# A two-layer decoder trunk on one core: the order of all instructions from a recorded list schedule in place of an online planner, and masked matmul steps at half width

## The chip, the core and the metric

The kernel runs on one core of one Trainium2 chip. The metric is the device time of one execution in microseconds (us); the time before is the median of three runs. One further execution was profiled: its trace gives, for every instruction, the engine, the start and the duration. The engines are PE (TensorE: matmuls and weight loads), DVE (VectorE), ACT (ScalarE), POOL (GpSimd) and SP (the engine that issues most DMAs).

## The reference, cut to what matters

Two layers over 2048 tokens of width 1024, all float32. Layer 0 is a gated DeltaNet with 8 heads (key width 128, value width 256), layer 1 a gated linear attention (GLA) with 4 heads of the same widths. Each layer projects its input, mixes along time, gates, projects back and normalises:

```
def gated_delta_rule(q, k, v, g, beta):
    ...
    A = jnp.where(strict, jnp.einsum('bhncd,bhnsd->bhncs', kb, k) * decay, 0.0)
    uw = lax.linalg.triangular_solve(A + eye, rhs, left_side=True, lower=True, unit_diagonal=True)
    ...
    def step(S, inp):
        v_new = u_n - jnp.einsum('bhcd,bhde->bhce', w_n, S)
        o = jnp.einsum('bhcd,bhde->bhce', qd_n, S) + jnp.einsum('bhcs,bhse->bhce', qk_n, v_new)
        S = S * gl_n[..., None, None] + jnp.einsum('bhcd,bhce->bhde', kd_n, v_new)
...
    x = layer_norm(DEEP_ALPHA * x + y, ln_g[i], ln_b[i])
```

Layer 0 also puts a causal convolution of four taps and a SiLU on q, k and v. GLA has the same recurrence without the triangular solve, with a decay per channel that makes its attention matrix a sum over levels of block pairs.

## The kernel before

**Tiling.** The tokens come in four groups of 512, each of four chunks of 128. A unit is one head of one layer on one group: 32 DeltaNet and 16 GLA units, in the order of `PHASES` (line 942): DeltaNet groups 0 and 1, GLA group 0, DeltaNet 2, GLA 1, DeltaNet 3, GLA 2, GLA 3. So there are seven changes of group.

**The work of a unit** is written as four kinds of steps.

- `gemms` (line 433) projects the inputs. Both operands are split into a high and a low part in float32r, and each product is three matmuls (`mm3`, line 235): by channel with 512 moving columns, by token with 256. The weights come in chunks through `wc` (16 buffers, line 933). The first time, a chunk is loaded raw (`wraw`), split by ACT and POOL and stored to DRAM as `wk`; later it is loaded split. The inputs `xh`, `xl` (8 buffers each) are reloaded at each change of group (`load_x`, line 377) through `woraw`, whose four buffers serve the output weights and the norm parameters too. Results leave PSUM through three buffers "g".
- `gdn_prep` (line 575) and `gla_prep` (line 677) prepare the chunk matrices in plain float32. DeltaNet inverts a unit triangular matrix: blocks of 16 by a loop of 15 steps on DVE (line 633), fed by a DMA that spreads the blocks over the partitions (`Arep`, line 627), and then doublings with matmuls. The doubling from 16 to 32 (lines 643 to 652) multiplies full 128x128 matrices and masks the result; those to 64 and 128 work on the blocks alone. GLA fills its attention matrix level by level; four levels (line 745) multiply full matrices and copy under a mask.
- `gdn_chain` and `gla_chain` (lines 790 and 815) run the recurrence over four chunks. Each DeltaNet chunk goes through PE, DVE, PE, ACT, PE and DVE in turn (`S`, `Rt`, `wt`). `chains` (line 828) then transposes the output.
- `outs` (line 855) multiplies by the output weights and, after a layer's last head, normalises. It has one PSUM buffer "o".

**The order.** The four kinds are generators that run as threads (line 929). `Plan.note` (line 70) estimates for each instruction when it ends, from the formulas of `COST` (line 131): for DVE 110 ns and 1.04 ns per element, for ACT 110 and 0.84, for POOL 90 and 2.35, and 800 ns until another engine may use the result. Each `yield` names a time; `Plan.run` (line 99) goes on with the first thread that is due on the planned clock of PE. Fixed times (`O_GAP`, `R_SLACK`, `AHEAD`, `Y_WAIT`) space some steps. The instructions are issued to the framework at once, in this order, and it may still reorder them; one instruction is pinned (`keep_in_program_order`, line 638).

Of the kernel before, what the change touches and what calls it, by code (L numbers as in the profile page):

```python
# [16 lines left out]
P = 128  # L17
# [33 lines left out]
class Plan:  # L51
# [3 lines left out]
    def __init__(self):  # L55
        self.clock = 0.0
        self.events = {}
        self.busy = dict.fromkeys("vsgd", 0.0)
        self.done, self.used, self.opens, self.slots = {}, {}, {}, {}

    def tile(self, tag, ap, bufs):
        slots = self.slots.setdefault(tag, [])
        slots.append(ap.tensor.name)
        self.opens[slots[-1]] = self.used.get(slots[-1 - bufs], 0.0) if len(slots) > bufs else 0.0

    def ready(self, *tiles):
        names = [t[:].tensor.name for t in tiles]
        return max(max(self.done.get(n, 0.0), self.opens.get(n, 0.0)) for n in names)

    def note(self, key, aps):  # L70
        dst, src = aps[0], aps[1:]
        names = [a.tensor.name for a in aps]
        t = max([self.opens.get(names[0], 0.0)] + [self.done.get(n, 0.0) for n in names[1:]])
        n = 1
        for k in (src[-1] if key == "t" else dst).shape[1:]:
            n *= k
        psum = any(a.space == PSUM for a in aps)
        if key == "t":
            m = 1
            for k in src[0].shape[1:]:  # L80
                m *= k
            rate = 0.6 if src[0].dtype == F32 else 2.4
            cost = m / 1.2 if src[0] is src[-1] else max(n / rate, m / rate, 107 if rate > 1 else 53)
            self.clock = end = max(self.clock, t) + cost
            end += COST["t"]
        else:
            if key == "d":
                cost, wait = COST["d"], COST["dw"] + 4 * n * P / 200
            else:
                fixed, each = COST[key]  # L90
                cost, wait = fixed + n * each, COST["w"]
            begin = max(self.busy[key], t)
            self.busy[key] = max(self.busy[key], min(begin, self.clock)) + cost
            end = begin + cost + wait
        self.done[names[0]] = max(end, self.done.get(names[0], 0.0))
        for a in names:
            self.used[a] = max(end, self.used.get(a, 0.0))

    def run(self, *threads, start):
        def due(th):  # L100
            return self.events.get(th[1], 1e30) if isinstance(th[1], tuple) else th[1]

        threads = [[t, t0] for t, t0 in zip(threads, start)]
        while threads:
            th = next((th for th in threads if due(th) <= self.clock), None) or min(threads, key=due)
            assert due(th) < 1e30
            self.clock = max(self.clock, due(th))
            try:
                th[1] = next(th[0])
            except StopIteration:  # L110
                threads.remove(th)


class Planned:
    def __init__(self, plan, engine, key):
        self.plan, self.engine, self.key = plan, engine, key

    def __getattr__(self, name):
        op = getattr(self.engine, name)

        def call(*args, **kw):
            ins = op(*args, **kw)  # L122
            aps = [a for a in (*args, *kw.values()) if isinstance(a, bass.AP)]
            if name == "transpose":
                aps = [aps[0], aps[1], aps[1]]
            self.plan.note(self.key, aps)
            return ins
# [7 lines left out]
def trunk(ctx, tc, x, xT, w_in1, conv, a_log, dt_bias, nw1, w_out1, w_in2, gk_up, gk_b, nw2, w_out2,  # L135
          ln_g, ln_b, consts, out, phases=None):
    nc = tc.nc
    plan = Plan()
    v, s, g = (Planned(plan, e, k) for e, k in ((nc.vector, "v"), (nc.scalar, "s"), (nc.gpsimd, "g")))
    pe, sync, acts = Planned(plan, nc.tensor, "t"), Planned(plan, nc.sync, "d"), Planned(plan, nc.scalar, "d")  # L140
    ready, events = plan.ready, plan.events
# [10 lines left out]
    def T(tag, shape, bufs=1, dt=F32, p=None):  # L152
        count[0] += 1
        t = (p or sb).tile(list(shape), dt, tag=tag, name=f"{tag}_{count[0]}", bufs=bufs)
        plan.tile(tag, t[:], bufs)
        return t
# [87 lines left out]
    def after(*names):  # L244
        for name in names:
            yield name

    def mark(*name):
        events[name] = plan.clock

    def prefetched(specs, load, ahead=1):
        ready = []
        specs = iter(specs)

        def take(ahead=ahead):
            while len(ready) <= ahead:
                spec = next(specs, None)
                ready.append(None if spec is None else load(spec))
            return ready.pop(0)
        return take  # L260

    class Stream:

        def __init__(self, specs):
            self.specs = iter(specs)
            self.chunks = {}
            self.taken = self.loaded = 0
            self.kept = {}  # L270

        def load(self, freed):
            while self.loaded < freed + W_BUFS:
                spec = next(self.specs, None)
                if spec is None:
                    return
                w, cols, kc, key, last = spec
                wc = T("wc", [P, 2, 272], W_BUFS, F32R)
                n = sum(2 * cn if pair else cn for c0, cn, pair in cols)
                if key in self.kept:  # L280
                    sync.dma_start(wc[:, :, :n].bitcast(F32), self.kept[key][:, :, :n])
                    self.chunks[self.loaded] = wc, None
                else:
                    raw = T("wraw", [P, 272], RAW_BUFS)
                    rows = w[kc * P:(kc + 1) * P]
                    n = 0
                    for c0, cn, pair in cols:
                        if pair:
                            sync.dma_start(raw[:, :2 * cn].rearrange("p (a b) -> p a b", a=2),
                                           rows[:, :2 * pair].rearrange("p (a b) -> p a b", a=2)[:, :, c0:c0 + cn])  # L290
                            n = 2 * cn
                        else:
                            sync.dma_start(raw[:, n:n + cn], rows[:, c0:c0 + cn])
                            n += cn
                    split(wc[:, 0, :n], wc[:, 1, :n], raw[:, :n], g)
                    keep = None
                    if not last:
                        keep = self.kept[key] = T("wk_%d_%d_%d_%d" % key, [P, 2, n], p=dr)
# [684 lines left out]
```

## Time and profile before

| what | value |
|---|---|
| three runs | 3163.24, 3164.54, 3171.97 us; median 3164.54 |
| profiled execution, own time | 3160.78 us |
| its span, first to last instruction | 3159.0 us |
| instructions in the trace | 51501, of them 18430 matmuls |
| mean granted TensorE clock | 0.989 |
| DMA traffic | 551.86 MB, 175 GB/s in the mean |

A row of a profile gives the engine, the operation with its output and inputs, the shape (stationary rows*columns, then moving partitions x elements), the count, the busy time with the mean duration, and idle time ahead of it with what ended it. All instructions have line 122, a helper's, so groups are told apart by tiles. A matmul's end is modelled: it is drawn longer than the time after which the next one can start. The pitch, from one matmul's start to the next, is what counts. A float32 matmul shows as two matmul instructions.

### The profile page before, as it was taken

Reading aid. Unit: us, or ns where it says so; the run is one execution under the profiler, and the core shown is the slowest. Engines: PE = TensorE matmul, PEld = TensorE weight load, DVE = VectorE, ACT = ScalarE, POOL = GpSimd, SP = SyncE. Lnnn points to the kernel's source line nnn. Section 1 sums busy time; section 2 is a strip of 40 time slices with the busy share of each in tenths; the row PEclk is TensorE's granted clock in tenths of the full one; section 3 lists DMA queues with packets and bytes.
Section 4 is the critical chain, followed back from the end, with each engine's and each line's share of the span. In section 5 each row is a group of like instructions: output and inputs, shape, how many; then the busy total and the mean of one; then the engine's idle time right before and its main releaser. Section 6 shows DMA issues by size and latency. Waiting matters only on the chain. (4 is left out here: it accounts for less than half of the span.)

```text
span 3159.0 us, 51501 instructions
## 1 busy us (share of the span) xinstructions
PE 3035.0 (96%) x18430; PEld 2591.3 (82%) x18430; DVE 2047.3 (65%) x4780; ACT 1184.4 (37%) x3091; POOL 519.2 (16%) x834
## 2 busy tenths in 40 slices
PE   8899999999999998999999999999999999999997
PEld 6678888778888887887888888888788888898886
DVE  5777777666666575567666657457866674745565
ACT  5445453343333445334233333423323332433331
POOL 5423330020001334002000001000200000200021
PEclk9999999999999999999999999999999999999998
DMA  7876665564444648655455444654645454455443
GB/s 238 258 230 220 191 216 185 165 214 138 141 147 152 212 132 280 215 175 196 135 157 161 142 149 134 206 179 154 198 151 154 139 161 132 157 188 170 151 161 107
DMA packets 442480, 551.86 MB, mean 175 GB/s; under 512 B 37568, under 2 KB 381888, under 8 KB 430192
## 3 DMA queue, kind: packets, MB, share of 16 engines
q1 hardware_dynamic: 412656, 505.57, 51.1%
q10 hardware_dynamic: 29568, 43.00, 3.9%
q8 instruction: 145, 2.38, 0.3%
q14 instruction: 111, 0.91, 0.1%
HBM read 421.24 MB, written 127.21 MB: 174 GB/s over the span
## 5 line engine op out<-in xcount | busy, mean ns | idle before, releaser
L122 PE MATMUL psg<-xh,wc 128*128 128x512 f32 x2560 | 890.1, 406 | 4.5 <-ACT wc L122 2.4
L122 PE MATMUL psg<-wc,xh 128*128 128x256 f32 (+1 forms) x4096 | 795.6, 291 | 10.0 <-POOL wc L122 2.5
L122 PEld LDWEIGHTS psg<-wc,xh 128*128 128x128 f32 x4096 | 658.8, 190 | 44.0 <-POOL wc L122 4.4
L122 PE MATMUL psg<-wc,xl 128*128 128x256 f32 (+1 forms) x2048 | 581.2, 284 | 0.4 <-DVE xl L122 0.4
L122 PEld LDWEIGHTS psg<-xh,wc 128*128 128x128 f32 x2560 | 482.1, 189 | 115.4 <-POOL wc L122 4.4
L122 PE MATMUL psg<-xl,wc 128*128 128x512 f32 x1280 | 514.8, 402 | 0.8 <-DVE xl L122 0.8
L122 PE MATMUL pso<-wo,oth 128*128 128x512 f32 x1472 | 505.1, 420 | 5.3 <-DVE y L122 4.6
L122 DVE SCALAR_TENSOR_TENSOR y<-pso,z,y 128x512 f32<-128x512 f32 x368 | 274.2, 745 | 193.8 <-PE pso L122 188.2
L122 PEld LDWEIGHTS psg<-wc,xl 128*128 128x128 f32 x2048 | 389.7, 190 | 1.8 <-DVE xl L122 0.9
L122 DVE SCALAR_TENSOR_TENSOR acc<-pb,taps,acc 128x512 f32<-128x512 f32 x384 | 302.8, 791 | 95.0 <-ACT acc L122 88.1
L122 PE MATMUL pso<-wo,otl 128*128 128x512 f32 x736 | 297.4, 404 | 0.0
L122 PEld LDWEIGHTS pso<-wo,oth 128*128 128x128 f32 x1472 | 254.3, 190 | 48.0 <-DVE y L122 13.0
L122 POOL TENSOR_TENSOR wc<-wraw,wc 128x256 fp32r<-128x256 f32 (+1 forms) x288 | 233.8, 825 | 323.5 <-ACT wc L122 313.2
L122 PEld LDWEIGHTS psg<-xl,wc 128*128 128x128 f32 x1280 | 242.2, 189 | 51.7 <-DVE xl L122 2.0
L122 ACT ACTIVATE junk<-psc 128x128 bf16<-128x128 f32 (+1 forms) x448 | 143.7, 321 | 230.0 <-PE psc L122 186.0
L122 ACT ACTIVATE th<-psg 128x256 f32<-128x256 f32 (+1 forms) x256 | 108.6, 436 | 254.2 <-PE psg L122 224.4
L122 ACT ACTIVATE D<-D 128x512 f32<-128x512 f32 x160 | 98.5, 630 | 212.5 <-DVE D L122 200.5
L122 PEld LDWEIGHTS pso<-wo,otl 128*128 128x128 f32 x736 | 138.8, 189 | 32.5 <-DVE otl L122 1.7
L122 DVE SCALAR_TENSOR_TENSOR sg<-th,psg 128x256 f32<-128x256 f32 x192 | 79.3, 417 | 124.0 <-ACT th L122 96.6
L122 ACT COPY pb<-psg 128x512 f32<-128x512 f32 x128 | 74.8, 584 | 224.6 <-PE psg L122 208.6
L122 ACT CAST wc<-wraw 128x256 fp32r<-128x256 f32 (+1 forms) x288 | 113.4, 406 | 121.0 <-PE psg L122 59.4
L122 DVE TENSOR_TENSOR Xt<-Arep,X 128x60 f32<-128x60 f32 (+14 forms) x480 | 103.3, 215 | 32.0 <-DMA Arep<-blk 22.0
(170 smaller groups left out, 4320.4 us busy)
## 6 DMA issues: line engine op xcount, KB each, us to landing
wc<-wk SPq DMA_DIRECT2D x816, 256.0 KB
wk<-wc SPq DMA_DIRECT2D x272, 256.0 KB
wraw<-in_w_in SPq DMA_DIRECT2D x288, 128.0 KB
wo<-ok_in_w_out SPq DMA_DIRECT2D x24, 1024.0 KB
wo<-k_in_w_out SPq DMA_DIRECT2D x24, 1024.0 KB
wo<-_in_w_out SPq DMA_DIRECT2D x22, 1024.0 KB
Arep<-blk SPq DMA_DIRECT2D x32, 512.0 KB
wc<-wk SPq DMA_DIRECT2D x48, 272.0 KB
```

Of the source, the lines that this page charges most:

```text
L122: ins = op(*args, **kw)
```

## The change

`Plan` and the threads go. Every instruction is recorded first (`Recorder.note`) with the tile regions that it reads and writes, then `place` decides the order of all of them, and `emit` issues them in that order, each pinned. `place` is a list scheduler: five queues (PE, DVE, ACT, POOL, and SP for DMAs), each takes the ready instruction of best rank: the chain first, then preparation, output, and projections last. An instruction that is the first to use a tile waits for a free buffer, in the order of the program within its rank, and its unit may be at most two ahead of the first unit whose chain is unfinished. The durations have new formulas per engine and operation; the result counts as there after a lag and 100 ns more (`SLACK`), 200 ns more for PE; a DMA lands 3500 ns and size/170 after its issue, `Arep` after 9000.

```diff
+        if key == "t":
+            mov = size_of(every[2].shape) if op.name == "matmul" else size_of(every[1].shape)
+            if op.name == "transpose":
+                op.cost = 2 * dst.shape[0] / 2.4 + 4
+            elif every[1].dtype == F32:
+                op.cost = 4 * mov / 2.4 + 9
+            else:
+                op.cost = mov / 2.25 + 4.5
+            op.lag = 210
+        elif key == "d":
+            size = 4 * n * dst.shape[0]
+            op.cost, op.lag = 430, DMA_LAG + size / 170
+            if isinstance(dst, View) and dst.of.tag == "Arep":
+                op.lag = REP_LAG
...
+        elif key == "v":
+            n = max(n, max(size_of(a.shape) for a in every))
+            took = (150 if psum else 160) + 1.04 * n
+            if op.name == "scalar_tensor_tensor":
+                took += 55
+            if len(every) > 2 and not psum and n > 64:
+                took *= 1.12
+            op.cost, op.lag = took - 80, 80 + LAG
+        elif key == "s":
+            took = (165 if psum else 210) + 0.833 * n
...
+            op.cost, op.lag = took - 95, 95 + LAG
         else:
...
+            took = 140 + 2.8 * n if len(every) > 2 else 300 + n
+            if op.args[-1] == ALU.pow:
+                took = 450 + 160 * n
+            op.cost, op.lag = took - 40, 40 + LAG
...
+            placed.append(op)
+            for u in op.users:
+                u.ready = max(u.ready, now + cost if u.deps[op] else end + (100 if u.key == "t" else 0) + SLACK)
...
+        for op in self.place():
+            tc.keep_in_program_order(op.call(*[real(a) for a in op.args], **{k: real(a) for k, a in op.kw.items()}))
...
-COST = {"v": (110, 1.04), "s": (110, 0.84), "g": (90, 2.35), "w": 800, "t": 200, "d": 450, "dw": 2000}
+LAG = 60
+DMA_LAG, REP_LAG, SLACK = 3500, 9000, 100
```

The masked steps work on the later half of each block pair alone: the stationary operand keeps its 128 columns, the moving one has 64, and the DVE steps on the result have 256 elements in place of 512.

```diff
+    def later_half(a, sz):
...
+        return a.rearrange("p n (m h j) -> p n m h j", h=2, j=sz)[:, :, :, 1, :]
...
-        d = PS("c", [P, NC, P])
-        yield ready(d, U)
+        Uh, Wh = later_half(U[:], 16), halves(W2[:, :, :P // 2], 16)
+        d = halves(PS("c", [P, NC, P // 2]), 16)
         for n in range(NC):
-            mm(d[:, n], A[:, n], U[:, n])
-        v.tensor_tensor(W2[:], d, bc(C(C_LV + 4), 1, NC), ALU.mult)
...
+            mm(d[:, n], A[:, n], Uh[:, n])
+        v.tensor_tensor(Wh, d, bc(later_half(C(C_LV + 4), 16), 1, NC), ALU.mult)
+        d = halves(PS("c", [P, NC, P // 2]), 16)
         for n in range(NC):
-            mm(d[:, n], Tm[:, n], W2[:, n])
-        v.tensor_tensor(U[:], U[:], d, ALU.subtract)
+            mm(d[:, n], Tm[:, n], Wh[:, n])
+        v.tensor_tensor(Uh, Uh, d, ALU.subtract)
...
+                d = halves(d, half)
+                E3 = E[:].rearrange("p (n t) -> p n t", n=NC)
                 for n in range(NC):
-                    c = slice(n * P, (n + 1) * P)
-                    mm(d[:, n], E[:, c], E[:, c])
-                v.copy_predicated(At[:], bc(C(C_LV + lv), 1, NC).bitcast(I32), d)
+                    mm(d[:, n], E3[:, n], later_half(E3, half)[:, n])
+                v.copy_predicated(later_half(At[:], half), bc(later_half(C(C_LV + lv), half), 1, NC).bitcast(I32), d)
```

Buffers and queues move too. Inputs get raw buffers of their own, two of them, and a load claims its `xh` and `xl` with its raw buffer; the output weights keep two raw buffers, the norm parameters get four. The stores of scaled output weights go from ACT's queue to SP's. The store of a split weight chunk no longer waits for the chunk's last use. The last unit's transposed output goes to `oth` and `otl` as every other unit's does. The loads of `y` lose their fixed delay; by rank they stand ahead of the projections' loads.

```diff
     def load_x(u, kc):
...
-        raw = T("woraw", [P, TG], WO_RAW_BUFS)
-        sync.dma_start(raw[:], x2T[u.gi][:, kc, :] if u.kind else xT[kc * P:(kc + 1) * P, u.t0:u.t0 + TG])
+        raw = T("xraw", [P, TG], 2)
         hi, lo = T("xh", [P, TG], KC, F32R), T("xl", [P, TG], KC, F32R)
+        sync.dma_start(raw[:], x2T[u.gi][:, kc, :] if u.kind else xT[kc * P:(kc + 1) * P, u.t0:u.t0 + TG],
+                       also=(hi, lo))
...
-            acts.dma_start(k[:], t[:].bitcast(F32))
...
+            sync.dma_start(kept_wo[key][:], t[:].bitcast(F32))
...
-                hi = T("D1" if end else "oth", [P, NC, P], 2, F32R)
+            hi = T("oth", [P, NC, P], 2, F32R)
...
-    plan.run(chains(), preps(), outs(), gemms(), start=(0.0, 0.0, 1.0, 0.0))
+    for u in units:
+        rec.unit = u.at
+        gemms(u)
+        preps(u)
+        chains(u)
+        outs(u)
+    rec.emit(tc)
...
-W_BUFS, RAW_BUFS = 16, 4
-WO_BUFS, WO_AHEAD, WO_RAW_BUFS = 2, 1, 4
+W_BUFS, RAW_BUFS = 14, 3
+WO_BUFS, WO_RAW_BUFS = 2, 2
...
-O_GAP = 7050
-R_SLACK, AHEAD = 2500, 500
-Y_WAIT = 20000
+R_CHAIN, R_PREP, R_OUT, R_GEMM = range(4)
+HORIZON = 2
```

More of the change, by code (lines that the diff above doesn't have):

```diff
@@ L262, in trunk @@
[L262 to L298, printed above, removed]
-                    self.chunks[self.loaded] = wc, keep
-                self.loaded += 1
-        def take(self):
-            self.taken += 1
-            return self.taken - 1, self.chunks.pop(self.taken - 1)
@@ L517, in short_conv @@
+        if not u.first:
+            gate(DV)
     def short_conv(d, blk):
@@ new lines, in chains @@
+    def chains(u):
+        rec.rank = R_CHAIN
+        og, ssq = T("og", [P, NC, DV], 1), small("ssq", NC)
+        (gdn_chain if u.kind == 0 else gla_chain)(u, og, ssq)
+        z = small("z", NC)
+        if u.kind == 1:
+            rsqrt(z[:], ssq[:], DV * 1e-6)
+        else:
+            v.tensor_tensor(ssq[:], ssq[:], u.prep["qn"][:], ALU.add)
+            rsqrt(z[:], ssq[:], 0.0)
+        u.z = z
+        u.oT = []
+        for j in range(2):
+            d = PS("c", [P, NC, P])
+            transposes(d, lambda n: og[:, n, j * P:(j + 1) * P], NC)
+            hi = T("oth", [P, NC, P], 2, F32R)
+            lo = T("otl", [P, NC, P], 2, F32R)
+            split(hi[:], lo[:], d)
+            u.oT.append((hi, lo))
```

713 lines of the change are left out of this document (398 added, 315 removed).

## The prediction

> **What bounds the kernel now.** I read the page first, then the groups by shape, the chain that ended last, the timeline, stretches of time, and the waits of PE's loads.
>
> ```profile
> span 3159.0 us, 51501 instructions
> ## 1 busy us (share of the span) xinstructions
> PE 3035.0 (96%) x18430; PEld 2591.3 (82%) x18430; DVE 2047.3 (65%) x4780; ACT 1184.4 (37%) x3091; POOL 519.2 (16%) x834
> ```
>
> PE looks 96% busy: 124 us of the span are idle. But ends of matmuls are modelled, so part of each wait is drawn as work. The pitch, start to start, tells what PE needs:
>
> ```profile
> 2285.41 5.60 PE psg L122 x24
> ...
> 2307.34 3.19 PE psg L122 x27
> ```
>
> ```profile
> 493.42 1.05 PE L122 MATMUL psc<-U,D 128*128 128x128 f32 x8
> ...
> 499.54 0.59 PE L122 MATMUL psc<-U,D 128*32 128x32 f32 x16
> ...
> 510.95 1.03 PE L122 MATMUL psc<-kq 128*128 128x256 f32 x4
> ```
>
> The first two rows are unbroken projection work: 5.60/24 = 233 ns with 512 moving columns, 3.19/27 = 118 ns with 256. In float32 the last matmul's drawn length comes off first (284, 199 and 381 ns in the groups): (1.05-0.284)/7 = 110 ns with 128 columns, (0.59-0.199)/15 = 26 ns with 32, (1.03-0.381)/3 = 216 ns with 256.
>
> ```profile
> L122 PE MATMUL psg<-xh,wc 128*128 128x512 f32 x2560 | 890.1, 406 | 4.5 <-ACT wc L122 2.4 <-POOL wc L122 1.2 <-ACT xh L122 0.7
> L122 PE MATMUL psg<-wc,xh 128*128 128x256 f32 x3584 | 690.1, 290 | 6.9 <-DVE sg L122 2.3 <-ACT vt L122 1.7 <-ACT wc L122 1.6
> L122 PE MATMUL psg<-xl,wc 128*128 128x512 f32 x1280 | 514.8, 402 | 0.8 <-DVE xl L122 0.8
> L122 PE MATMUL psg<-wc,xl 128*128 128x256 f32 x1792 | 505.5, 282 | 0.0
> L122 PE MATMUL pso<-wo,oth 128*128 128x512 f32 x1472 | 505.1, 420 | 5.3 <-DVE y L122 4.6
> L122 PE MATMUL pso<-wo,otl 128*128 128x512 f32 x736 | 297.4, 404 | 0.0
> L122 PE MATMUL psc<-S,qd 128*128 128x256 f32 x384 | 115.4, 382 | 0.6 <-DVE qn L122 0.6
> ...
> L122 PE MATMUL psc<-D 128*128 128x128 f32 x512 | 68.6, 277 | 2.8 <-DVE otl L122 2.4 <-DVE D L122 0.3
> ...
> L122 PE MATMUL psc<-cst,og 128*128 128x128 f32 x384 | 58.8, 275 | 9.9 <-DVE og L122 8.4 <-DVE D L122 1.5
> L122 PE MATMUL psh<-vt,kd 128*128 128x256 f32 x128 | 41.2, 404 | 7.7 <-DVE S L122 7.6
> L122 PE MATMUL psc<-vt,D 128*128 128x256 f32 x128 | 39.4, 390 | 0.8 <-ACT D L122 0.8
> ...
> L122 PE MATMUL psc<-W,Tm 128*128 128x128 f32 x256 | 35.6, 284 | 3.5 <-DVE W L122 3.5
> L122 PE MATMUL psc<-U,D 128*128 128x128 f32 x256 | 35.5, 284 | 7.6 <-DVE U L122 7.6
> ```
>
> Counts by pitch: 6048 of 512 columns (and 96 in small groups) by 0.232 are 1425 us. 6144 of 256 (768 of them slightly wider) by 0.118 to 0.125 are 730. 1920 in float32 with 256 columns (eight groups, the first and last shown) by 0.216 are 415. The 1024 masked ones (`D`, `W,Tm`, `U,D`) by 0.110 are 113, 1104 transposes by 0.109 are 120, and 2100 small ones some 106. The sum is 2909 us: PE needs 2909 of 3159 and loses 250, twice what the page shows as idle. This is the whole of what an order can win. Where it is lost:
>
> ```profile
> 0.00:200.00 200.00, 174.47 (x932) 139.72 (x932) 131.68 (x283) 93.98 (x264) 88.95 (x131) 0.96 0.81 254
> 200.00:3100.00 2900.00, 2821.26 (x17322) 2420.22 (x17323) 1879.85 (x4438) 1079.79 (x2806) 415.99 (x685) 0.99 0.54 171
> 3100.00:3159.00 59.00, 39.24 (x177) 31.32 (x176) 35.77 (x63) 10.63 (x22) 14.28 (x18) 0.86 0.19 72
> ```
>
> The columns are the stretch, its length, PE, PEld, DVE, ACT and POOL busy, clock, DMA share and GB/s. Idle as drawn: 25.5 us in the first 200, where DMA is 0.81 busy; 78.7 in the middle; 19.8 in the tail. Summed by pitch over the matmuls of each stretch, the losses are 47, 183 and 20.
>
> ```profile
> sum 350.00, PE 311.93 PEld 265.62 DVE 266.32 ACT 152.21 POOL 120.88; mean PE 44.56 PEld 37.95 DVE 38.05 ACT 21.74 POOL 17.27
> ```
>
> ```profile
> PEld psh L122 <- DVE S L122: 42.4, 68, 2.8
> PEld psh L122 <- ACT wt L122: 21.4, 79, 4.4
> PEld psh L122 <- DVE Rt L122: 16.6, 36, 2.3
> ```
>
> The sum row is over seven stretches of 50 us, around or soon after a layer's normalisation: 38 of the middle's 78.7 us are there. The waits are short and many: 183 hand-overs of the recurrence alone (`S`, `wt`, `Rt`), 80 us in all, 0.44 each. They come of an order that put the next matmul too early, with nothing else between.
>
> **The change part by part.**
>
> *The order.* The planner before costed the state's update at 110+1.04*256 = 376 ns and the power on POOL at 90+2.35*4 = 99 ns.
>
> ```profile
> L122 DVE SCALAR_TENSOR_TENSOR S<-S,eg,psh 128x256 f32<-128x256 f32 x128 | 60.9, 476 | 61.3 <-PE psh L122 60.2 <-PE psc L122 0.2
> ```
>
> ```profile
> L122 POOL TENSOR_TENSOR z<-ssq,mhalf 128x4 f32<-128x4 f32 x32 | 34.5, 1078 | 323.5 <-DVE ssq L122 271.1 <-DVE X L122 24.0 <-ACT pb L122 9.4
> ```
>
> The new formulas give 150+1.04*256+55 = 471 (traced 476) and 450+160*4 = 1090 (1078); a 512-column matmul is 232 ns (traced 233) where the old one had 213. So the plan knows when a result is there, and SLACK puts the next matmul later than that, with projection matmuls between. They are the lowest rank and always at hand: a unit has about 45 us of projections in its 2909/48 = 61 us. What can go is the middle's 183 us. I leave 65: 1.5 us per 100 where a queue is pinned and an estimate is off, and 3 to 4 us at each of seven group changes. Gain: 118.
>
> The first 200 us: `y`'s loads rank ahead of the projections' inputs. 2 MB at the stretch's 254 GB/s are 8 us ahead of the first projection. Inputs then come through two raw buffers. As the loads are the same in sum, and DMA is busy 0.81 of the stretch, I take 6 us of loss, between -20 (a better order) and +25. The tail stays at 20: the last normalisation has nothing to hide behind.
>
> *Half-width steps.* 1024 matmuls move 64 columns in place of 128, with the stationary operand still 128 wide. By the moving width a pitch would go from 110 to about half, some 58 ns: 1024*0.052 = 53 us. One row speaks against it, a matmul with 128 stationary and 32 moving columns:
>
> ```profile
> 46.68 0.53 PE L122 MATMUL psc<-lgz,cst 128*128 128x32 f32 x4
> 47.04 0.46 PE L122 MATMUL psh<-S,kq 128*128 128x256 f32 x1
> ```
>
> Four took (47.04-46.68)/4 = 90 ns each, and (0.53-0.276)/3 = 85 by the drawn ends (276 is the last one's length), where 32 stationary with 32 moving columns took 26. Both contain one short first step, drawn early after another kind of matmul; without it, the rest are near 110. So the stationary width sets the pitch here, and I take 0 of 53. [...]
>
> On DVE they save about 1 us per unit, of 2047 in all: off the path. The planner does believe in the saving (4*64/2.4+9 = 116 ns per float32 matmul, where two steps of 110 are 220), so after each such group of four PE is 0.4 us behind the plan. SLACK is 0.1 us, so DVE waits 0.3 us; PE has projections behind it. I put that in the 65.
>
> *Buffers and queues.* Two of 16 weight buffers less, and three raw ones: a chunk serves 1.4 us of PE, so 14 are some 20 us of lead; nothing, but if a load lands later than that PE waits. The moved stores cost SP 24 issues; it waits on PE most of the time. At nothing.
>
> **The sum.** Span 3159 - 118 + 6 = 3047, own time 3160.8 - 112 = 3049. The median of the runs lies 3.8 above the profiled execution, so some 3052; I say 3050.
>
> **The rivals.**
>
> 1. *Half-width pays.* If the moving width decides after all, 53 us more go: 2997. For it speaks that nothing shows 64 moving against 128 stationary columns; against it the row above. [...] 0.08.
> 2. *The plan is met nearly to the ns.* 183 go to 25 and the start is as before: 3159 - 158 = 3001, so some 3005. Against it: pinned queues have no way round an error. 0.14.
> 3. *Inputs through two buffers.* A raw buffer is held from issue over the cast to the subtraction:
>
> ```profile
> 4.57 0.62 ACT L122 CAST xh<-woraw 128x512 fp32r<-128x512 f32 x1 [1.18 <-DMA woraw<-in_xT]
> 5.21 0.69 DVE L122 TENSOR_TENSOR xl<-woraw,xh 128x512 fp32r<-128x512 f32 x1 [0.53 <-ACT xh L122]
> ```
>
>  With a landing of 3.5 us, as the plan has it, that is 4.8 us per use: eight chunks in 19 us with two buffers, 10 with four. If PE has nothing else then, it loses 9 us at each of eight groups: 72, and 3122. For it: a load now waits for its `xh` and `xl` too. Against: outputs and chains are left as fill. 0.20.
> 4. *Pinned and late (slower).* Each engine issues in the planned order, so a late result stops all behind it. A DeltaNet unit has about 21 hand-overs to PE, a GLA unit 14: 32*21+16*14 = 896. From 3050 there are 124 us to lose until the time is 0.3% over the old (3174): 0.14 us each, beyond what SLACK covers. Before lost 0.44 at 183 of them. Should transfers come late as well, 0.2 each gives 3050+179 = 3229; just past the point, 3185. 0.12.
> 5. *The framework's own order already did this* and the time stays within 0.3%: against it the 250 us lost. 0.06.
>
> **How the numbers follow.** The forecast (3025 to 3085) has 0.40. A measurement of this kernel tells 0.3% from no change, here 3155 to 3174. Faster: 0.40+0.08+0.14+0.20 = 0.82, same 0.06, slower 0.12. The range goes from 2985, which takes in rivals 1 and 2 but not their sum, to 3155, which takes in rival 3 and leaves out 4 and 5: 0.82 of the chance.
>
> **What would show it.** Right: PE's idle in the middle falls from 78.7 to some 30 us with PE's instruction count the same, the waits on `S`, `wt`, `Rt` under 30 us, and the masked matmuls at a pitch near 110 ns. Wrong: a pitch near 58 (rival 1); idle on `xh` and `xl` at each group's start (rival 3); waits of PE on DVE and ACT as many as before, in other places (rival 4).

## The result, and the profile after

| | before | after |
|---|---|---|
| median of the runs shown with the result | 3163.98 us (4 runs, 3163.24 to 3171.97) | 3213.59 us (4 runs, 3210.70 to 3217.51) |
| profiled execution, span | 3159.0 us | 3215.7 us |
| granted TensorE clock | 0.989 | 0.978 |

The ratio is 1.0152, 95% interval 1.0132 to 1.0172. The change made the kernel 48 us slower, and the forecast was 3050, 114 us faster. Below, 1% of ratio is 31.6 us; experiments are compared by their ratios to the kernel before, which ran beside each of them.

The head of the page of after:

```profile
span 3215.7 us, 51309 instructions
## 1 busy us (share of the span) xinstructions
PE 3058.7 (95%) x18430; PEld 2602.5 (81%) x18430; DVE 2046.4 (64%) x4780; ACT 1171.3 (36%) x3091; POOL 523.3 (16%) x834
```

PE has the same 18430 matmuls. It was idle 3159.0-3035.0 = 124.0 us before and 3215.7-3058.7 = 157.0 after: 33 us more. And the same matmuls were busy 3058.7-3035.0 = 23.7 us longer: a slower clock. In the stretches that the records of the clock give at half, PE was drawn busy 94 us after and 48 before, on matmuls that by pitch need 48 and 26; the difference of these excesses, 24 us, is the whole of it. Idle and clock together are the 56.7 us between the spans. By stretches (length, PE, PEld, DVE, ACT, POOL busy, clock, DMA share, GB/s):

```profile
0.00:200.00 200.00, 162.40 (x832) 129.41 (x832) 124.03 (x286) 85.51 (x246) 72.76 (x112) 0.90 0.69 219
200.00:3100.00 2900.00, 2801.17 (x16975) 2388.48 (x16974) 1864.08 (x4379) 1054.74 (x2779) 435.77 (x704) 0.99 0.55 171
3100.00:3215.00 115.00, 95.10 (x628) 84.57 (x627) 58.32 (x118) 31.05 (x69) 14.73 (x18) 0.93 0.31 97
```

PE does 12 us less in the first 200 us than before (162.40 for 174.47), and idles 98.8 us in the middle where 78.7 stood and 30 were forecast. The waits say where. For PE's weight loads (total us, times, longest), first one row of before and then after:

```profile
PEld pso L122 <- DVE y L122: 13.0, 26, 1.9
```

```profile
PEld pso L350 <- DVE y L350: 28.2, 56, 1.7
PEld psg L350 <- ACT xh L350: 26.9, 11, 12.2
...
PEld psg L350 <- DVE xl L350: 14.8, 7, 4.3
...
PEld psh L350 <- DVE S L350: 11.4, 20, 1.2
...
PEld psh L350 <- DVE Rt L350: 7.2, 18, 0.6
PEld psh L350 <- ACT wt L350: 6.8, 13, 1.0
```

The waits of the recurrence on `S`, `wt` and `Rt` did fall: 80.4 us in 183 waits became 25.4 in 51. In their place stand others. Those on `xh` and `xl`, the split inputs, rose from 7.7 us to 41.7; they are few and long, 22.8 us of them at the start and the rest around the changes of group. All other waits of these loads on DVE and ACT rose from 90 us in 130 waits to 143 in 228, those on `y` among them. So with the inputs left aside, PE's loads waited on DVE and ACT 171 us in 313 waits before and 169 in 279 after: the hand-overs moved more than they went. The seven stretches of 130 us from just before each reload of the inputs, summed, first before and then after:

```profile
sum 910.00, PE 891.66 PEld 770.49 DVE 548.73 ACT 324.98 POOL 72.59; mean PE 127.38 PEld 110.07 DVE 78.39 ACT 46.43 POOL 10.37
```

```profile
sum 910.00, PE 829.72 PEld 709.63 DVE 598.02 ACT 360.32 POOL 170.56; mean PE 118.53 PEld 101.38 DVE 85.43 ACT 51.48 POOL 24.37
```

PE is idle 18 us of the 910 before and 80 after. Summed by pitch, as the prediction did (span less count times pitch), the loss is:

| us lost | first 200 | seven reload stretches | last 100 | all the rest | sum |
|---|---|---|---|---|---|
| before | 47 | 51 | 21 | 129 | 248 |
| after | 61 | 142 | 24 | 79 | 306 |

By this split the rest got better by 50 us, and the reload stretches took back 91 and the start 14. But the stretches do not hold the same work in both kernels. The normalisation that ends a group (its first `lnmr` is taken as its start) comes 138 to 158 us after the first cast of the reload in before, outside the stretch, and 20 to 55 us after it in after, inside. Seven stretches of 70 us, from 10 us before each normalisation on, summed, for before, after and after_x_once (an experiment below, without reloads):

```profile
sum 490.00, PE 453.43 PEld 396.29 DVE 352.71 ACT 212.59 POOL 154.89; mean PE 64.78 PEld 56.61 DVE 50.39 ACT 30.37 POOL 22.13
```

```profile
sum 490.00, PE 435.01 PEld 362.27 DVE 356.37 ACT 225.94 POOL 145.73; mean PE 62.14 PEld 51.75 DVE 50.91 ACT 32.28 POOL 20.82
```

```profile
sum 490.00, PE 455.92 PEld 387.52 DVE 366.06 ACT 232.57 POOL 146.98; mean PE 65.13 PEld 55.36 DVE 52.29 ACT 33.22 POOL 21.00
```

PE is idle 37, 55 and 34 us there, and by pitch it loses 65, 85 and 59 (these sums and the table agree within some 3 us). Without the normalisations the rest loses 4.6 us per 100 before and 4.1 after: the order won some 10 us there, not 50. What is left of the reload stretches loses 54 us of 910 before and 59 of 420 after.

Here is one reload in the timeline of after, first SP's queue, then ScalarE's casts and some of PE's matmuls:

```profile
554.00 3.17 SPq L350 DMA_DIRECT2D wc<-wk  x5
557.27 1.02 SPq L350 DMA_DIRECT2D xraw<-in_xT  x2
...
563.49 12.90 SPq L350 DMA_DIRECT2D xraw<-in_xT  x4
...
555.00 0.61 ACT L350 CAST xh<-xraw 128x512 fp32r<-128x512 f32 x1
...
562.12 0.62 ACT L350 CAST xh<-xraw 128x512 fp32r<-128x512 f32 x1 [3.60 <-DMA xraw<-in_xT]
563.20 0.62 ACT L350 CAST xh<-xraw 128x512 fp32r<-128x512 f32 x1
572.36 0.60 ACT L350 CAST xh<-xraw 128x512 fp32r<-128x512 f32 x1
573.16 0.63 ACT L350 CAST xh<-xraw 128x512 fp32r<-128x512 f32 x1
...
559.06 1.10 PE L350 MATMUL psc<-W,Tm 128*128 128x64 f32 x8 [0.52 <-DVE W L350]
560.71 0.71 PE L350 MATMUL psc<-U,D 128*32 128x32 f32 x16 [0.55 <-DVE U L350]
562.79 1.50 PE L350 MATMUL psg<-wc,xh 128*128 128x272 f32 x5 [1.38 <-ACT xh L350]
```

The casts go in pairs (the first of the first pair, at 553.58, is left out), from 554, 562 and 572, and again from 582: two raw buffers, some 9 us per round. From the first cast to the last, eight chunks took 23 to 29 us in the seven reloads; before, 11 to 22. The plan itself has a round of this length: an input of 256 KB lands 3500 ns and size/170, so 5.0 us, after its issue there, and with a cast of 0.62 and a subtraction of 0.69 a raw buffer is held 6.3 us. Four rounds are 25 us. In the trace the 13 casts that show a wait for their input began 3.0 to 6.7 us after its issue; the other 51 show none, so for these the landing was not what came last. SP stands 12.9 us with four loads, as each may go only when DVE has read a raw buffer:

```profile
SPq L350 <- DVE xl L350: 48.6, 31, 6.7
```

And the clock in the same place:

```profile
556.00:558.00 2.00, 2.00 (x17) 1.78 (x16) 1.38 (x3) 0.89 (x2) 0.00 (x0) 1.00 1.05 383
558.00:560.00 2.00, 1.48 (x13) 1.35 (x12) 1.42 (x3) 0.52 (x1) 0.00 (x0) 1.00 1.07 361
560.00:562.00 2.00, 0.87 (x18) 0.60 (x17) 1.37 (x3) 0.00 (x0) 0.00 (x0) 0.75 1.13 426
562.00:564.00 2.00, 1.21 (x5) 1.18 (x5) 0.84 (x2) 1.65 (x4) 0.00 (x0) 0.50 1.00 418
564.00:570.00 6.00, 6.00 (x43) 5.10 (x42) 0.85 (x2) 0.90 (x3) 0.00 (x0) 0.50 0.37 108
570.00:576.00 6.00, 4.94 (x18) 3.65 (x18) 1.74 (x3) 3.18 (x9) 0.00 (x0) 0.50 0.17 41
576.00:579.00 3.00, 3.00 (x14) 2.69 (x14) 0.95 (x3) 0.28 (x2) 0.00 (x0) 0.65 0.33 93
```

The mean of 0.75 from 560 to 562 is full clock up to 561 and half from there, for some 17 us, in which PE looks busy but the matmuls come further apart: 227 ns with 272 moving columns, 125 at full clock (medians of this trace). Ahead of the fall stand two gaps of 0.52 and 0.55 us, on `W` and `U` of the preparation; from 557.4 on no projection stands beside it, and the wait of 1.38 us on `xh` begins at 561.4, just after the fall. By pitch some 12 us are lost from 557.4 to 578.1, of which 3.5 are drawn as gaps; the rest shows as busy time. So this stretch without projections cost over three times its drawn gaps.

### The profile page after: what moved, and what is told of

Same layout as the page of the kernel before. It is cut to its first block, busy times and chain, and to the rows that moved or that the text cites. A ratio compares the mean times of both kernels' runs of the same rounds, so it can differ in the third digit from the quotient of the medians.

```text
span 3215.7 us, 51309 instructions
## 1 busy us (share of the span) xinstructions
PE 3058.7 (95%) x18430; PEld 2602.5 (81%) x18430; DVE 2046.4 (64%) x4780; ACT 1171.3 (36%) x3091; POOL 523.3 (16%) x834
## 4 chain that ended last, share of the span: by engine, by line
PE 53%; DVE 5%; DMA 2%; ACT 2%; issue 1%; POOL 0%; SPq 0%; ACTq 0%; DVEq 0%
PE psg L350 30%; PE psc L350 10%; PE pso L350 9%; PE psh L350 3%; DVE y L350 1%; DMA x2T<-th 1%; DVE D L350 1%; DVE lnst L350 1%; DVE kd L350 0%; DMA xraw<-x2T 0%; ACT junk L350 0%; DVE acc L350 0%; DMA gcT<-gcT 0%; DMA Gb<-gcT 0%; DVE W L350 0%
## 5 line engine op out<-in xcount | busy, mean ns | idle before, releaser
L350 PE MATMUL psg<-xh,wc 128*128 128x512 f32 x2560 | 900.5, 416 | 31.4 <-ACT xh L350 18.6
L350 PE MATMUL psg<-wc,xh 128*128 128x256 f32 (+1 forms) x4096 | 813.0, 292 | 13.4 <-ACT xh L350 4.1
L350 PE MATMUL psg<-wc,xl 128*128 128x256 f32 (+1 forms) x2048 | 597.5, 295 | 12.3 <-DVE xl L350 12.3
L350 PE MATMUL psg<-xl,wc 128*128 128x512 f32 x1280 | 529.0, 414 | 0.1
L350 PE MATMUL pso<-wo,oth 128*128 128x512 f32 x1472 | 469.4, 399 | 13.6 <-DVE y L350 12.1
L350 PEld LDWEIGHTS psg<-wc,xl 128*128 128x128 f32 x2048 | 390.5, 192 | 21.3 <-DVE xl L350 12.9
L350 POOL COPY halo<-pb 128x3 f32<-128x3 f32 x128 | 29.1, 227 | 812.3 <-ACT pb L350 811.8
```

What stands on the lines that cost most here:

```text
L350: tc.keep_in_program_order(op.call(*[real(a) for a in op.args], **{k: real(a) for k, a in op.kw.items()}))
```

## The experiments

The theories: A, the lost time is PE left without inputs, at the start and at the seven reloads, and the half clock after that. B, the pinned queues and late hand-overs cost everywhere. C, half-width steps harm, since the plan counts on a saving that PE does not make. D, the units' chains of hand-overs outlast the work beside them. E came later: the planner's ranks use that work up before a group ends.

### Is it the pinning, or the slack?

**unpinned**: `emit` issues in the same order without the pin.

```diff
-            tc.keep_in_program_order(op.call(...))
+            op.call(...)
```

> The changed kernel with the same recorded order, but no instruction pinned, so that the framework may reorder each engine by its own estimates. Theory B, pinned queues stop behind late results: some of the loss goes, and the time falls by 15 us or more, to under 3200. Theory A, the inputs' two buffers and the idle time that the order itself holds: pinning is not the cause, and the time is within 12 us of 3214 or higher.

3364.54 us, ratio 1.0647 (1.0631 to 1.0663): 157 us slower than with the pin. The waits of the recurrence come back:

```profile
PEld psh L350 <- DVE S L350: 61.5, 43, 5.4
```

So the pin is worth much to this order, and is not the cause of the loss.

**slack0** and **slack300**: `SLACK` 0 and 300 in place of 100.

> The changed kernel with SLACK at 0 in place of 100 ns: in the recorded order each dependent step is put 0.1 us sooner. Theory D, the units' chains of hand-overs are so long that PE runs out of other work, and slack adds to them: 20 to 50 us go, to 3165 to 3195. Theory B, late results behind which pinned queues stop: less slack means more such waits, and the time rises by 15 us or more, to over 3228.

> The changed kernel with SLACK at 300 ns in place of 100. Theory D: slower by 50 us or more, to over 3264. Theory B: the waits of PE on DVE and ACT shrink, and the time falls by 15 us or more, to under 3200.

3213.52 us, 1.0171 (1.0154 to 1.0188), not told apart from after; and 3232.78, 1.023 (1.0214 to 1.0245), 25 us slower. By pitch, slack 300 loses 95 in the reload stretches (142 in after) and 144 in the rest (79); but four of its seven normalisations come 107 to 124 us after the reload's first cast, at the end of the stretch or behind it, and around the normalisations it loses 94 where after loses 85. Neither theory's numbers were met; the slack is not the lever. That the pin makes the loss is out. Late hand-overs cost about as much as before, by the waits above, so they do not explain the 48 us either.

### Is it the half width?

**full_width** (after with the masked steps at full width) and **before_half** (before with them at half width):

```diff
-            mm(d[:, n], A[:, n], Uh[:, n])
+            mm(d[:, n], A[:, n], U[:, n])
```

> The changed kernel with the masked steps at full width again. Theory A: the half width saves nothing on PE, so the pitch of the masked matmuls is 110 ns here as well, and the time is within 12 us of the changed kernel's 3214. Theory C, the half-width steps do harm, since the plan counts on 55 us that PE does not save and every queue is then early: the time falls by 25 us or more, to 3190 or less.

> The kernel before with the half-width masked steps alone, in the order of its own planner. Theory A: PE needs as long as before, and the time is within 12 us of 3164. Theory C, strided halves cost PE or DVE more than they save: slower by 15 us or more. If the moving width did set the pitch after all: some 50 us faster, 3110.

3203.86 us, 1.0128 (1.0113 to 1.0143), where after had 1.0152: 8 us the better, the intervals just overlapping. 3169.82 us, 1.0015 (1.0006 to 1.0025): 5 us slower than before. So half width brings nothing. It costs a little in the kernel before; in after the intervals do not tell.

**pitch_right**: the planner's price of a float32 matmul alone, set as traced:

```diff
-                op.cost = 4 * mov / 2.4 + 9
+                op.cost = 4 * max(mov, size_of(every[1].shape)) / 2.4 + 9
```

> Only the planner's cost of a float32 matmul is changed, to the larger of its moving and stationary columns, so that a half-width step is planned at 222 ns as traced. Theory B, and theory C (half-width steps harm because the plan counts on a saving that PE does not make): the drift of PE against the plan goes and the time falls by 10 us or more, to 3195 to 3204. Theory A: the group changes stay as they are, 3208 to 3216.

3236.17 us, 1.0223 (1.021 to 1.0237): 22 us slower with the truer price, which neither theory had. The reload stretches lost 157 in place of 142. The wrong price was not what cost the time.

### Is it the inputs?

**shared4**: inputs go through four raw buffers again, shared with the output weights.

```diff
-        raw = T("xraw", [P, TG], 2)
+        raw = T("woraw", [P, TG], WO_RAW_BUFS)
...
-WO_BUFS, WO_RAW_BUFS = 2, 2
+WO_BUFS, WO_RAW_BUFS = 2, 4
```

> The changed kernel, with the inputs again through the four raw buffers that they share with the output weights (no other edit, same memory). Theory A, inputs through two raw buffers starve PE at the start and at each change of group, and the idle time then halves the granted clock: the eight reloads of inputs fall from 25 to 29 us each to 11 to 20, the time at half clock from 141 us to under 100, PE's loads' waits on xh from 27 us to under 12, and the time by 60 to 100 us, to 3115 to 3155. Theory B, pinned queues lose a little at every hand-over, all through the run: no more than 15 us go, and the time stays over 3195.

3183.45 us, 1.0063 (1.0044 to 1.0082): 28 us of the 48 back, between what A and B expected. Six of the seven reloads now take 10 to 12 us, one 22, in place of 23 to 29, and their stretches lose 107 in place of 142.

**before_x2**: the opposite cut, two raw buffers for the inputs (and one weight buffer less) in the kernel before.

> The kernel before with the inputs through two raw buffers of their own in place of the shared four, and one weight buffer less for the room (15 for 16). Theory A: the reloads stretch from 11 to 21 us to over 18 each, and the time rises by 15 to 60 us, to 3180 to 3225. Theory B: the two buffers do no harm, and the time is within 10 us of 3164.

3177.09 us, 1.0035 (1.002 to 1.0049): 11 us slower, between what A and B expected. Its reloads stretch to 18 to 23 us, yet their stretches lose only 4 us more than before: a long reload alone does not starve PE. Most of what its trace loses more lies around the normalisations (79 for 65). At its first reload the old order issues the first load at 452 and casts from 497.8 to 511.6, and PE has projections of the old group until 503.9; in after the loads come from 534.9, the casts from 553.6, and the old group's projections end at 554.4.

**x2_other_tile**: in after, ScalarE stops behind its stores of the transposed `x2T`, whose two buffers it shares with the tanh of the projections, and PE behind ScalarE:

```profile
645.77 0.63 ACT L350 ACTIVATE th<-acc 128x512 f32<-128x512 f32 x1 [3.05 <-DMA x2T<-th]
647.16 0.69 ACT L350 ACTIVATE acc<-psg,taps 128x512 f32<-128x512 f32 x1 [0.76 <-DVE kq L350]
...
647.90 0.80 PE L350 MATMUL psg<-xh,wc 128*128 128x512 f32 x1 [6.43 <-ACT acc L350]
```

```diff
-                    xt = T("th", [P, 4, P], 2)
+                    xt = T("gb", [P, 4, P], 4)
```

> The copies of the normalised transpose on their way to x2T take the four buffers of another tile (gb) instead of the two that they share with the planner's other th tiles; all else as in the changed kernel. Theory A in its wider form (ScalarE stops behind the stores of x2T and PE with it): the stops of PE of 3 to 6 us after each of the four normalisations of the first layer go, 3195 to 3206. If those stops are covered elsewhere: 3210 to 3216.

3197.32 us, 1.0107 (1.0092 to 1.0122): 14 us better, as expected of A's wider form. These stops lie in the reload stretches too.

**inputs4_free**: four input buffers of their own (12 weight buffers), no early claim of `xh` and `xl`, the other tile for `x2T`, and the price of pitch_right, together.

> The changed kernel with four raw input buffers of their own, two weight buffers less for the room (12 for 14), input loads that no longer claim their split buffers, the transposed copies of the first layer's output in the norm parameters' four buffers instead of the two that the gates use, and the masked matmuls costed by their stationary width. Theory A: the lost time around the seven reloads falls from 142 us to under 80, and the time to 3110 to 3150, under that of the kernel before. Theory B: the losses move elsewhere, and the time stays over 3175.

3172.43 us, 1.0032 (1.0018 to 1.0046): 38 of the 48 us back, but not the 3110 to 3150 of A. The reload stretches still lost 96. The early claim of `xh` and `xl` was never taken away by itself, so its own part is not known.

**after_x_once** and **before_x_once**: the inputs are loaded and split for the first group alone, and every group computes with these, so the reloads are left out, and with them the second layer's wait for `x2T`; the values computed are not the reference's, but PE's work is the same.

```diff
-        u.G = group.setdefault((u.kind, u.gi), {"x": ([], [])})
+        u.G = group.setdefault((u.kind, u.gi), {"x": inputs})
```

> The changed kernel with the inputs xh and xl loaded and split for the first group alone; every later group computes with these (the reloads, their casts and subtractions, and the dependence of the second layer on x2T are left out; PE's work is the same). The changed kernel lost 142 us in the seven stretches of 130 us around the reloads; at the rate of the rest of its span (79 us in 2006) they would have lost 36. Theory A (the reload is what starves PE there): nearly all of the 106 goes, 3100 to 3125. Theory E (PE starves there since the planner ranks the chains first and the work beside them, projections above all, has run out at a group's end, or since the new unit's preparation is serial): at most a third goes, 3175 to 3205.

> The same cut in the kernel before. Theory A and theory E alike: its seven stretches lost 51 us, about the rate of the rest of its span, so nothing is to be won: 3150 to 3166. If it falls by more than 20 us, the reload costs both kernels and the comparison with the changed kernel has to go by the difference.

3150.70 us, 0.9963 (0.9951 to 0.9975), and 3158.40 us, 0.9977 (0.9968 to 0.9986). So the reload, that wait included, costs the changed kernel 1.89%, 60 us, and the kernel before 0.23%, 7 us. The difference, 53 us, is all of the 48 that the change lost; without reloads the two orders differ by 0.14%, which the intervals do not tell apart. The page of after_x_once:

```profile
span 3148.5 us, 51017 instructions
...
PE 3030.3 (96%) x18430; PEld 2586.0 (82%) x18430; DVE 2005.5 (64%) x4724; ACT 1135.5 (36%) x3035; POOL 519.9 (17%) x834
```

PE's idle is 118.2 us there, 39 less than after, and its busy time 28 less, some 18 of it by the clock: the slower clock went with the idle. Neither A's 3100 nor E's 3175 was met. A holds for what the change lost; it was wrong that nearly all of the reload stretches' loss was the reload's. Some 45 us of the 106 there are something else. Their place is the normalisation: by pitch these seven stretches still lose 59 us without reloads, where the old kernel loses 65, outside its reload stretches.

### Is it the start?

After issues 2 MB of `y` and the output weights ahead of the first input, and the first projection starts at 17.22 us (5.4 before):

```profile
0.72 1.81 SPq L350 DMA_DIRECT2D y<-in_x  x4
2.58 0.97 SPq L350 DMA_DIRECT2D woraw<-in_w_out  x2
...
8.09 0.33 SPq L350 DMA_DIRECT2D xraw<-in_xT  x1
...
17.22 1.22 PE L350 MATMUL psg<-xh,wc 128*128 128x512 f32 x2 [11.79 <-ACT xh L350]
...
27.37 1.22 PE L350 MATMUL psg<-xh,wc 128*128 128x512 f32 x2 [4.86 <-ACT xh L350]
```

**y_late**: the loads of `y` get the rank of the projections (`rec.rank = R_GEMM` around `load_y`).

> The loads of y are ranked with the projections instead of the outputs; all else as in the changed kernel. Theory A (lost time is PE left without inputs at the start and at the seven group changes, and the half clock that follows): the first projection comes some 8 us earlier, the loss of the first 200 us falls from 61 towards the 47 of before, and nothing changes at the group changes: 3200 to 3206. Theory B (late hand-overs all over the span): the start is worth nothing that can be measured, 3210 to 3216.

3211.51 us, 1.0145 (1.0132 to 1.0159): no change that can be told. The timeline of y_late says why:

```profile
11.95 1.22 PE L350 MATMUL psg<-xh,wc 128*128 128x512 f32 x2 [5.88 <-ACT xh L350]
...
24.52 1.22 PE L350 MATMUL psg<-xh,wc 128*128 128x512 f32 x2 [7.35 <-ACT xh L350]
```

The first projection came 5.3 us earlier and the next gap grew by 2.5: `y` is now issued between the first inputs, which go through two raw buffers here as well.

### Which version is best?

**all_four**: inputs4_free with y_late.

> Four input buffers of their own with 12 weight buffers, no early claim of xh and xl, copies to x2T in other buffers, the cost of float32 matmuls as traced, and y's loads ranked late, together. Theory A: the run with the first four stood at 3172, 41 under the changed kernel; a start as before takes another 8 to 14: 3158 to 3166, level with the kernel before. Theory B and D (the chains of hand-overs in each unit): the start adds nothing, 3169 to 3176.

3171.29 us, 1.0018 (1.0009 to 1.0026): 42 of the 48 us back, still a little slower than before. The start added nothing, as B and D had it.

**prep_first**: all_four with the ranks of chain and preparation exchanged.

```diff
-R_CHAIN, R_PREP, R_OUT, R_GEMM = range(4)
+R_PREP, R_CHAIN, R_OUT, R_GEMM = range(4)
```

> The version with all four repairs, and the preparation of a unit ranked ahead of the chains (one line). Theory E: the preparation of the next group's first unit no longer waits behind the chains and PE has more beside it at a group change: 3145 to 3163, under the kernel before. Theory A: the order of these two ranks changes nothing that can be measured, 3166 to 3178.

3159.22 us, 0.9977 (0.9968 to 0.9986): 13 us better by one line, as E expected, and ahead of the kernel before. But the reload stretches lost 92 where all_four lost 91; the gain is in the rest (88 to 75). So E's place was wrong; that a unit's preparation was late everywhere would fit, but is not shown.

**before_costs**: the old planner with five prices as traced (VectorE 155 for 110, 55 more for three operands, ScalarE 190 for 110, POOL's power, 2.25 columns per ns).

> The kernel before with nothing changed but five prices of its own planner, set as traced: VectorE 155 instead of 110 ns fixed, 55 more for the three-operand form, ScalarE 190 instead of 110, POOL's power 450+160 per column, and 2.25 instead of 2.4 columns per ns in the projections. If true durations are worth something by themselves (as the prediction had it: the order puts the next matmul too early), the waits on S, wt and Rt fall and the time with them: 3120 to 3150. If it is the list order and the pinning that took those waits away: 3155 to 3175.

3169.66 us, 1.0016 (1.0007 to 1.0025). The waits hardly fell (66 us in place of 80):

```profile
PEld psh L126 <- DVE S L126: 34.1, 57, 2.7
PEld psh L126 <- ACT wt L126: 24.2, 87, 2.1
...
PEld psh L126 <- DVE Rt L126: 8.0, 27, 0.5
```

So these five prices alone are worth nothing in the old order. As the waits come back without the pin (unpinned), it was the list order with its pin that took them away.

**start_held**: prep_first, with the first group's `y` and the first output weights held by a one-column copy from the first unit's values.

> On the version with the four repairs and preparation first (3159): the first group's loads of y and the first unit's output weights are held until that unit's value projection is there, by a one-column copy that each of them waits for. Theory A for the start (2.5 MB that nothing needs yet land among the first inputs and weights, since the planner gives every transfer a fixed time however many are under way): the loss of the first 200 us falls from 59 to 47 to 50 and the time to 3147 to 3153. If the start is bound by its own chains: 3156 to 3162.

3147.70 us, 0.9957 (0.9945 to 0.9969): 6 us better, the intervals touching. The first projection started at 9.99 us, yet the first 200 us still lost 55; most of the gain lies at the reloads (92 to 80). The place expected is thus not confirmed, and the start's last 8 us over the old kernel's stay unexplained.

**prep_full**: prep_first with the masked steps at full width.

> The same base with the masked steps at full width again; its planner costs a float32 matmul the same for both widths, so PE's plan is the same but for VectorE's part. Theory C as it was put (half width harms because the plan counts on a saving on PE that is not there): here it is not counted on, so no difference, 3156 to 3163. If the half-width form costs by itself (the kernel before was 5 us slower with it): 3148 to 3155.

3142.04 us, 0.9935 (0.9918 to 0.9953): 13 us better, and the fastest of all, 0.65% under the kernel before.

```profile
span 3141.7 us, 51300 instructions
...
PE 3025.3 (96%) x18430; PEld 2590.7 (82%) x18430; DVE 2063.1 (66%) x4780; ACT 1175.4 (37%) x3091; POOL 520.4 (17%) x834
```

Idle 116.4 us, busy 33 less than after. That makes three pairs in which half width is the slower (5, 8 and 13 us, the 8 within the intervals), the last with a planner that prices both alike. C as it was put is out; why the form costs is open. No pitch of PE shows it: in the last pair the loss is in the reload stretches (92 against 74), nearly all of it around the normalisations (73 against 58), as if the orders merely fell differently.

## Why the prediction was wrong, step by step

**Right.** That PE needs 2909 us by count and pitch, and that this is the frame: after needs 2909 too. That the waits on `S`, `wt` and `Rt` would be under 30 us (25.4). The tail (24 for 20). And the half-width steps: 0 of 53 us on PE. Groups of eight in after:

```profile
118.83 1.80 PE L350 MATMUL psc<-U,D 128*128 128x64 f32 x8
...
1043.42 1.00 PE L350 MATMUL psc<-U,D 128*128 128x64 f32 x8
```

```profile
L350 PE MATMUL psc<-U,D 128*128 128x64 f32 x256 | 33.0, 273 | 1.6 <-DVE U L350 1.6
```

(1.00-0.273)/7 = 104 ns with 64 moving columns; the median pitch in these groups over the trace is 112. Rival 1 is out. The first row is the same group under a lowered clock:

```profile
118.00:125.00 7.00, 7.00 (x38) 6.90 (x37) 2.98 (x7) 0.16 (x1) 0.03 (x1) 0.56 0.41 127
```

**Wrong: "I leave 65" of the middle's 183.** It was 221. Three things were in it.

- *"1.5 us per 100 where a queue is pinned and an estimate is off"* was 3.9 per 100 (79 us in 2006). The kernel before has 6.6 by the same split, but its normalisations lie in it; with these taken out of both it is 4.6 and 4.1, some 10 us. This is the step that failed: the gain of 118 supposed that PE's waits go once the plan knows when a result is there. Those on `S`, `wt` and `Rt` did go, 55 us, but other waits on DVE and ACT rose by 53, and without reloads the two orders differ by 0.14% (after_x_once, before_x_once).
- *"3 to 4 us at each of seven group changes"* was 20 lost per stretch, 15 over the rate of the rest, though each stretch holds a normalisation, which costs the old kernel some 9. The reason given, projections *"always at hand"*, fails just there: at a reload the projections are what PE waits for. Nor are they 45 us of a unit's 61: that counts the output's matmuls, which rank above them, and by the prediction's own counts and pitches the lowest rank has (891+730)/48 = 34. The reload is worth 60 us in all (after_x_once), 28 of it due to the raw buffers (shared4). Of the rest of these stretches 14 us are the stops behind `x2T` (x2_other_tile); each was measured singly, and they may overlap.
- *Nothing for the clock.* Of the 57 us between the spans 24 are the same matmuls at a lower clock. The row of before in the prediction has a clock of 0.96 in the first 200 us, and I read no price from it.

**Start +6**: 14. Its cause was named (`y` ahead of the inputs), but moving `y` alone gave nothing; two raw buffers hold the inputs back there as well. After 17 us the loss is only partly explained.

**Rival 3** (inputs through two buffers, 72 us, 0.20) named the mechanism, but that its price lies near the 60 us of the whole reload is luck: 72 was for two buffers against four, and that step measured 28 (shared4). Its round was too short as well: the landing of 3.5 us left out the plan's size/170, and with 5.0 a use is 6.3 us and eight chunks take 25 us, not 19; they took 23 to 29. I subtracted it from a gain of 112 that was not there, so it seemed to end at 3122. Its condition, *"if PE has nothing else then"*, is fulfilled: the outputs and chains named against it did not cover the 23 to 29 us of a reload. **Rival 4** (pinned and late) had the sign and the range, 3185 to 3229, but not the cause: without the pin it is 157 us worse. Its sign, waits on DVE and ACT as many as before in other places, nearly came (279 for 313, inputs aside); but they lose no more than before, so they take away the gain and do not make the 48 us. **Rival 2** and **rival 5** did not come.

What stays open: why a normalisation costs about as much in both orders (65 us before, 59 in after_x_once); what the early claim of `xh` and `xl` costs by itself; the start's remainder; the cost of the half-width form; and why truer prices made the list order slower. Orders of one planner differ by 10 to 20 us with no mechanism that the traces show, so a single small step here proves little alone.

## What to carry to other kernels

A list order and its pins are only as good as the supply: before trusting a fill, ask at which places the fill itself is what waits, and price each buffer there as a round (issue, landing, every reader) times the chunks over the buffers. Price a wait of PE by its length and by the clock after it (here 33 us more idle, and 24 us by the clock). When losses are split by stretches, see that a stretch holds the same work in both kernels: a normalisation that had moved from one stretch to another looked here like 50 us won. When a large rewrite moves a little, take away one resource in both kernels (here the reload): the difference of the two falls is the part that the change lost.

## What the runs showed of the hardware

In after the granted clock fell at 561.0 with only short gaps drawn ahead of it. In the rows above some 1.07 us of drawn idle stand in the 3.41 us ahead of the fall, in gaps of 0.52 and 0.55 us; the gap of 1.38 came after it. 6 us with PE drawn busy throughout (564 to 570) did not bring the clock back; it returned after some 17 us. All half-clock stretches in the records of the clock in before, after and prep_full, but for the last one that runs to the end, last 3.41 us or a multiple of it: 55 us in all before, 126 after, 58 in prep_full. The matmul ends in a trace are modelled, so the true gaps may be longer than drawn.
